# Hand-set waits, fixed buffers and two issuing engines in a batched product of 512x64 matrices

## Chip, cores and metric

Each run is on one core of one Trainium2 chip. The metric is the device time of one execution in microseconds (us); a median stands with the lowest and highest run.

## The reference

```python
x, y: float32 [8, 12, 512, 64]
np.einsum('bhtc,bhsc->bhts', x, y).astype(np.float32)   # 96 products of 512x64 by 64x512
```

25.17 MB are read and 100.66 MB written. Each load and each store of the kernel moves 2.097 MB; there are 12 loads and 48 stores.

## The kernel before

Inputs come into one of five 16 KB-per-partition slots, are cast to bf16, mixed, and transposed by VectorE. For each of 48 results TensorE makes two PSUM tiles, ScalarE evicts them into a slot, and SyncE stores the slot. Buffers come from pools, and the framework sets the waits.

```python
slots = ctx.enter_context(tc.tile_pool(name="slots", bufs=SLOTS))          # SLOTS = 5
pmpool = ctx.enter_context(tc.tile_pool(name="pmpsum", bufs=2, space=bass.MemoryType.PSUM))
...
def result(o, otf):
    i, h = divmod(o, V)
    xT, yT = made[i]
    ot = otf.rearrange("p (r s) -> p r s", s=S)
    for k in range(0, K, 4):
        pm = pmpool.tile([P, 4, S], fp32)
        for j in range(4):
            nc.tensor.matmul(pm[:, j, :], xT[:, k + j, h, :], yT[:, h * S:(h + 1) * S], ...)
        copy(nc.scalar, ot[:, k:k + 4, :], pm)
    nc.sync.dma_start(ov[i, h], otf)
...
with tc.manual_schedule():
    for g in range(SLOTS):
        load(g)
    ...                                   # casts, mixes, loads 5 to 11, results 0 to 3
    for o in range(V, V * NH):            # results 4 to 47
        result(o, slot())
        ...
```

## Time and profile before

| | before |
|---|---|
| time, median of the first 3 runs | 301.13 us (301.11 to 301.54) |
| span of the profiled execution | 299.4 us |
| busy share PE / VectorE / ScalarE / GpSimd | 46% / 52% / 71% / 19% |
| share of the transfer engines' time in the one queue | 98.8% |
| mean rate over the span | 420 GB/s |

The two rows to read together are the last ones: no compute engine is full, the transfers are.

### The profile page before, as it was taken

What the parts mean: (1) busy time and instruction counts of PE and PEld (TensorE: products, weight loads), DVE (VectorE), ACT (ScalarE), POOL (GpSimd) and SP (SyncE); (2) the same over time, 40 slices, a digit from 0 to 9 for tenths busy, and PEclk for the clock granted to TensorE, in tenths of its full rate; (3) what the DMA queues carried; (4) which work ended last, traced back from release to release, by engine and by line L of the source; (5) the groups of instructions that cost most, each with busy time, mean ns of one, the idle gap of its engine ahead of it and who ended that gap; (6) DMA issues with size and microseconds to landing.
All of it is one profiled execution on the core that took longest, in us unless ns stands there. A gap on an engine that the chain in (4) does not pass through costs nothing.

```text
span 299.4 us, 1218 instructions
## 1 busy us (share of the span) xinstructions
PE 136.7 (46%) x377; PEld 45.3 (15%) x384; DVE 154.5 (52%) x80; ACT 211.8 (71%) x109; POOL 56.6 (19%) x38
## 2 busy tenths in 40 slices
PE   0000130555665555746666466657465756465000
PEld 0000010111222221212112122212121212121000
DVE  2259996999749592916719359086192520000000
ACT  1756576999999978686867777777777686868100
POOL 3399989991000000000000000000000000000000
PEclk9999999978799997595677776677787577676555
DMA  7999999999999999999999999999999999999995
GB/s 282 431 433 429 429 427 431 429 425 436 431 427 433 431 425 430 440 424 427 440 425 427 442 422 429 437 425 431 427 431 429 425 429 425 429 422 427 429 431 219
DMA packets 8646, 125.91 MB, mean 421 GB/s; under 512 B 960, under 2 KB 960, under 8 KB 960
## 3 DMA queue, kind: packets, MB, share of 16 engines
q1 hardware_dynamic: 8640, 125.83, 98.8%
q8 instruction: 3, 0.05, 0.1%
q14 instruction: 3, 0.02, 0.0%
HBM read 25.17 MB, written 100.66 MB: 420 GB/s over the span
## 4 chain that ended last, share of the span: by engine, by line
DMA 55%; ACT 21%; DVE 7%; issue 5%; PE 2%; ACTq 1%; SPq 0%
DMA out_dram<-slot 48%; ACT slot L66 20%; DMA slot<-in_y_dram 7%; DVE yb L68 6%; PE pm L133 2%; DVE xT L115 1%; ACT yb L66 1%; ACTq L201 1%; DVE yT L120 1%; SPq L75 0%; ACTq L66 0%; ACT xk L83 0%
## 5 line engine op out<-in xcount | busy, mean ns | idle before, releaser
L66 ACT ACTIVATE slot<-pm 128x2048 f32<-128x2048 f32 x96 | 174.2, 1887 | 44.0 <-DMA out_dram<-slot 42.3
L133 PE MATMUL pm<-yT,xT 128*128 128x512 bf16 x377 | 136.7, 504 | 137.9 <-ACT slot L66 100.8
L115 DVE STREAM_TRANSPOSE xT<-xb 128x2048 uint32<-128x2048 uint32 x12 | 46.7, 3894 | 68.4 <-PE pm L133 68.3
L133 PEld LDWEIGHTS <-xT 128*128 128x128 bf16 x384 | 45.3, 118 | 228.5 <-issue 177.8
L68 DVE COPY xb<-xk 32x2048 bf16<-32x2048 bf16 x36 | 46.9, 1303 | 0.5
L68 DVE CAST yb<-slot 64x2048 bf16<-64x2048 f32 x12 | 38.5, 3204 | 16.8 <-DMA slot<-in_y_dram 16.6
L68 POOL COPY xb<-xk 32x2048 bf16<-32x2048 bf16 x12 | 37.3, 3107 | 9.6 <-ACT xk L83 8.9
L83 ACT ACTIVATE xk<-slot 128x4096 bf16<-128x4096 f32 x6 | 21.7, 3617 | 16.1 <-DMA slot<-in_x_dram 16.1
L120 DVE STREAM_TRANSPOSE yT<-yb 128x1024 uint32<-128x1024 uint32 x12 | 23.1, 1927 | 0.0
L66 ACT ACTIVATE yb<-slot 64x2048 bf16<-64x2048 f32 x6 | 14.8, 2462 | 5.1 <-DMA slot<-in_y_dram 5.1
L68 POOL CAST yb<-slot 64x2048 bf16<-64x2048 f32 x6 | 16.8, 2808 | 1.5 <-DMA slot<-in_y_dram 1.4
L152 DVE MEMSET xb<- 128x256 uint32 x8 | 2.2, 272 | 0.9 <-PEq L190 0.9
L152 POOL MEMSET xb<- 128x128 uint32 x16 | 2.3, 210 | 0.3 <-POOLq L190 0.3
L83 ACT ACT_TABLE_LOAD x1 | 1.3, 1283 | 0.7 <-PEq L190 0.7
L190 POOL MEMSET const-float32-0.0<- 128x1 f32 x1 | 0.1, 98 | 0.2 <-issue 0.2
L190 POOL MEMSET const-float32-1.0<- 128x1 f32 x1 | 0.1, 98 | 0.0
L190 POOL MEMSET const-bfloat16-1.0<- 128x1 bf16 x1 | 0.1, 98 | 0.0
L190 POOL MEMSET const-uint8-127<- 128x1 uint8 x1 | 0.1, 98 | 0.0
## 6 DMA issues: line engine op xcount, KB each, us to landing
out_dram<-slot SPq DMA_DIRECT2D x48, 2048.0 KB, 20.6
slot<-in_x_dram SPq DMA_DIRECT2D x6, 2048.0 KB, 16.4
slot<-in_y_dram SPq DMA_DIRECT2D x6, 2048.0 KB, 20.8
```

Source lines behind the costliest of these rows:

```text
L66: nc.scalar.activation(dst, src, COPY)
L68: engine.tensor_copy(dst, src)
L83: nc.scalar.activation(xk.rearrange("p r c -> p (r c)"), src, COPY)
L115: nc.vector.transpose(xT.rearrange("p (k r e) -> p k e r", k=K, e=E), xb.rearrange("p (k e c) -> p k e c", k=K, e=E),)
L120: nc.vector.transpose(yT.rearrange("p (r j) -> p j r", r=D), yb.rearrange("p (j c) -> p j c", c=D))
L133: nc.tensor.matmul(pm[:, j, :], xT[:, k + j, h, :], yT[:, h * S:(h + 1) * S], start=True, stop=True)
L152: engine.memset(zeroed[half][:, k:k + part], 0.0)
L190: nc = _bacc.Bacc("TRN2", target_bir_lowering=False, num_devices=1)
L201: with _tile.TileContext(nc) as tc:
```

## The change

The intent: drop waits that another wait already implies, know each buffer by name, and share the issuing of stores between SyncE and ScalarE. Cut to its core:

```diff
-    slots = ctx.enter_context(tc.tile_pool(name="slots", bufs=SLOTS))
-    ...
+    slots = [sb.tile([P, K * S], fp32, name=f"slot{i}") for i in range(SLOTS)]
+    ...                                       # the other pools likewise, same counts
+    def need(name, points):                   # wait only for counts not yet known,
+        ...                                   # or not implied by another wait of the same list
+    def emit(name, make, reads=(), writes=(), dma=None): ...
+    def by_act(o):
+        return o % 3 == 2 or o >= V * NH - V
     def result(o, s):
         for k in range(0, K, 4):
-            copy(nc.scalar, ot[:, k:k + 4, :], pm)
-        nc.sync.dma_start(ov[i, h], otf)
+            emit("pe", lambda: products(o, k), ...)
+            copy("dve" if o in late else "act", ot[:, k:k + 4, :], pms[pm], ...)   # late: results 43, 47
+            if k == 0:
+                while later:
+                    store(*later.pop())       # a ScalarE store goes behind the next
+        if by_act(o):                         # result's first eviction
+            later.append((o, s))
+        else:
+            store(o, s)
-    with tc.manual_schedule():
+    with tc.tile_critical():
         ...
+        for i, name in enumerate(("dve", "pool", "dve", "pe", "act")):
+            need(name, [(f"dma{i}", ticks[f"dma{i}"])])
```

More of the change, by code (lines that the diff above doesn't have):

```diff
@@ L52 @@
     )
-    const = ctx.enter_context(tc.tile_pool(name="const", bufs=1))
-    kept = ctx.enter_context(tc.tile_pool(name="kept", bufs=NG - 1))
-    slots = ctx.enter_context(tc.tile_pool(name="slots", bufs=SLOTS))
-    tpool = ctx.enter_context(tc.tile_pool(name="tpool", bufs=2))
-    pmpool = ctx.enter_context(tc.tile_pool(name="pmpsum", bufs=2, space=bass.MemoryType.PSUM))
-    loaded, inputs, mixed, made = {}, {}, {}, {}
-    zeroed = [const.tile([P, K * E * D], u32, name=f"xb{half}") for half in range(2)]
@@ L62 @@
-    in_front = [nc.vector, nc.gpsimd, nc.vector, nc.scalar]
-    def copy(engine, dst, src):
-        if engine is nc.scalar:
-            nc.scalar.activation(dst, src, COPY)
-        else:
-            engine.tensor_copy(dst, src)
+    sb = ctx.enter_context(tc.tile_pool(name="sb", bufs=1))
+    ps = ctx.enter_context(tc.tile_pool(name="ps", bufs=1, space=bass.MemoryType.PSUM))
+    slots = [sb.tile([P, K * S], fp32, name=f"slot{i}") for i in range(SLOTS)]
+    xks = [sb.tile([P, R, C], bf16, name=f"xk{i}") for i in range(NG - 1)]
@@ new lines @@
+    ybs = [[sb.tile([P, R // 2 * D], u32, name=f"yb{h}{i}") for i in range(NG - 1 + h)] for h in range(2)]
+    xbs = [sb.tile([P, K * E * D], u32, name=f"xb{half}") for half in range(2)]
+    xTs = [sb.tile([P, K * D * E], u32, name=f"xT{i}") for i in range(2)]
+    yTs = [sb.tile([P, D * R // 2], u32, name=f"yT{i}") for i in range(2)]
+    pms = [ps.tile([P, 4, S], fp32, name=f"pm{i}") for i in range(2)]
+    engines = {"act": nc.scalar, "dve": nc.vector, "pool": nc.gpsimd, "pe": nc.tensor, "sp": nc.sync}
@@ new lines @@
+    sems, ticks, known, snaps, writer, readers = {}, {}, {e: {} for e in engines}, {}, {}, {}
+    def need(name, points):
+        best = {}
+        for p, v in points:
+            if known[name].get(p, 0) < v:
+                best[p] = max(best.get(p, 0), v)
+        for p, v in list(best.items()):
+            if any(snaps[q, w].get(p, 0) >= v for q, w in best.items() if q != p):
+                del best[p]
+        for p, v in best.items():
+            engines[name].wait_ge(sems[p], v)
+            known[name][p] = v
+            for q, w in snaps[p, v].items():
+                known[name][q] = max(known[name].get(q, 0), w)
@@ new lines, in emit @@
+    def emit(name, make, reads=(), writes=(), dma=None):
+        points = [writer[r] for r in (*reads, *writes) if r in writer]
+        points += [v for w in writes for v in readers.get(w, ())]
+        if name == "pool" and name in ticks:
+            points.append((name, ticks[name]))
+        need(name, points)
+        p, step = (name, 1) if dma is None else (f"dma{dma}", 16)
+        if p not in sems:
+            sems[p] = tc.alloc_semaphore(p)
+        make().then_inc(sems[p], step)
+        at = (p, ticks.get(p, 0) + step)
+        ticks[p] = at[1]
+        snaps[at] = {**known[name], p: at[1]}
+        if dma is None:
+            snaps[at][name] = at[1]
+        for r in reads:
+            readers.setdefault(r, []).append(at)
+        for w in writes:
+            writer[w], readers[w] = at, []
@@ L70, in slot, with copy, both @@
+    made_slots, loaded, later, late = [], {}, [], (V * NH - V - 1, V * NH - 1)
+    in_front = ["dve", "pool", "dve", "act"]
+    def copy(name, dst, src, reads, writes):
+        emit(
+            name,
+            lambda: nc.scalar.activation(dst, src, COPY)
+            if name == "act"
+            else engines[name].tensor_copy(dst, src),
+            reads,
+            writes,
+        )
+    def both(i):
+        return [("slot", i, 0), ("slot", i, 1)]
     def slot():
-        return slots.tile([P, K * S], fp32, name="slot")
+        made_slots.append(len(made_slots) % SLOTS)
+        return made_slots[-1]
@@ L73, in load @@
     def load(n):
-        loaded[n] = slot()
-        nc.sync.dma_start(loaded[n], (yv if n % 2 else xv)[n // 2])
+        i = loaded[n] = slot()
+        emit(
+            "sp",
+            lambda: nc.sync.dma_start(slots[i], (yv if n % 2 else xv)[n // 2]),
+            writes=both(i),
+            dma=i,
+        )
     def compress(n):
-        src = loaded.pop(n)
+        i = loaded.pop(n)
         g = n // 2
         if n % 2 == 0:
-            xk = kept.tile([P, R, C], bf16)
-            nc.scalar.activation(xk.rearrange("p r c -> p (r c)"), src, COPY)
-            inputs[g] = xk
+            xk = g % (NG - 1)
+            dst = xks[xk].rearrange("p r c -> p (r c)")
+            copy("act", dst, slots[i], both(i), [("xk", xk)])
@@ L85, in compress @@
             return
-        ys = src.rearrange("p (r c) -> p r c", c=C)
+        ys = slots[i].rearrange("p (r c) -> p r c", c=C)
         for half in range(2):
-            yb = kept.tile([P, R // 2 * D], u32, name=f"yb{half}", bufs=NG - 1 + half)
-            yv2 = yb.bitcast(bf16).rearrange("p (j c w) -> p j w c", j=R // 2, w=2)
+            b = g % (NG - 1 + half)
+            yv2 = ybs[half][b].bitcast(bf16).rearrange("p (j c w) -> p j w c", j=R // 2, w=2)
             for ch in range(2):
@@ L96, in compress, with mix @@
                     ),
-                )
-            mixed[2 * g + half] = yb
-    def mix(i, engine, part):
+                    both(i),
+                    [("yb", half, b, ch)],
+                )
+    def mix(i, name, part):
         g, half = divmod(i, 2)
@@ L104, in mix @@
         lo = half * 64 + u * D
-        xv2 = zeroed[half].bitcast(bf16).rearrange("p (k e c u) -> p k e c u", k=K, e=E, u=2)
+        xk = g % (NG - 1)
+        xv2 = xbs[half].bitcast(bf16).rearrange("p (k e c u) -> p k e c u", k=K, e=E, u=2)
         copy(
-            engine,
+            name,
             xv2[part * D:(part + 1) * D, :, :, :, u],
-            inputs[g][lo:lo + D, :, ch * D:(ch + 1) * D].rearrange("p (e k) c -> p k e c", k=K),
+            xks[xk][lo:lo + D, :, ch * D:(ch + 1) * D].rearrange("p (e k) c -> p k e c", k=K),
+            [("xk", xk)],
+            [("xb", half, part)],
@@ L110, in mix @@
         )
     def transposes(i):
-        xb, yb = zeroed[i % 2], mixed.pop(i)
-        xT = tpool.tile([P, K * D * E], u32)
-        nc.vector.transpose(
-            xT.rearrange("p (k r e) -> p k e r", k=K, e=E),
-            xb.rearrange("p (k e c) -> p k e c", k=K, e=E),
-        )
-        yT = tpool.tile([P, D * R // 2], u32)
-        nc.vector.transpose(
-            yT.rearrange("p (r j) -> p j r", r=D), yb.rearrange("p (j c) -> p j c", c=D)
-        )
-        made[i] = (xT.bitcast(bf16).rearrange("p (k h m) -> p k h m", k=K, h=V), yT.bitcast(bf16))
@@ L125, in result @@
-    def result(o, otf):
+        g, half = divmod(i, 2)
+        b = g % (NG - 1 + half)
+        emit(
+            "dve",
+            lambda: nc.vector.transpose(
+                xTs[half].rearrange("p (k r e) -> p k e r", k=K, e=E),
+                xbs[half].rearrange("p (k e c) -> p k e c", k=K, e=E),
+            ),
+            [("xb", half, part) for part in range(4)],
+            [("xT", half)],
+        )
+        emit(
+            "dve",
+            lambda: nc.vector.transpose(
+                yTs[half].rearrange("p (r j) -> p j r", r=D),
+                ybs[half][b].rearrange("p (j c) -> p j c", c=D),
+            ),
+            [("yb", half, b, ch) for ch in range(2)],
+            [("yT", half)],
+        )
@@ L127, in result, with products @@
+    def products(o, k):
         i, h = divmod(o, V)
-        xT, yT = made[i]
-        ot = otf.rearrange("p (r s) -> p r s", s=S)
-        for k in range(0, K, 4):
-            pm = pmpool.tile([P, 4, S], fp32)
-            for j in range(4):
-                nc.tensor.matmul(
-                    pm[:, j, :], xT[:, k + j, h, :], yT[:, h * S:(h + 1) * S], start=True, stop=True
-                )
-            copy(nc.scalar, ot[:, k:k + 4, :], pm)
-        nc.sync.dma_start(ov[i, h], otf)
+        xT = xTs[i % 2].bitcast(bf16).rearrange("p (k h m) -> p k h m", k=K, h=V)
+        yT = yTs[i % 2].bitcast(bf16)
+        for j in range(4):
+            last = nc.tensor.matmul(
+                pms[k // 4][:, j, :], xT[:, k + j, h, :], yT[:, h * S:(h + 1) * S],
+                start=True, stop=True,
+            )
+        return last
@@ new lines, in by_act, with store, result @@
+    def by_act(o):
+        return o % 3 == 2 or o >= V * NH - V
+    def store(o, s):
+        i, h = divmod(o, V)
+        name = "act" if by_act(o) else "sp"
+        emit(
+            name,
+            lambda: engines[name].dma_start(ov[i, h], slots[s]),
+            reads=both(s),
+            dma=s,
+        )
+    def result(o, s):
+        ot = slots[s].rearrange("p (r s) -> p r s", s=S)
+        for k in range(0, K, 4):
+            pm = k // 4
+            half = o // V % 2
+            emit("pe", lambda: products(o, k), [("xT", half), ("yT", half)], [("pm", pm)])
+            copy("dve" if o in late else "act", ot[:, k:k + 4, :], pms[pm], [("pm", pm)], [("slot", s, pm)])
+            if k == 0:
[5 more added lines that the diff above has]
+            store(o, s)
@@ L144, in prepare @@
             for part in range(4):
-                mix(i + 1, nc.vector, part)
-    with tc.manual_schedule():
+                mix(i + 1, "dve", part)
+    with tc.tile_critical():
         for g in range(SLOTS):
             load(g)
-        for half, engine, part in ((0, nc.vector, 256), (1, nc.gpsimd, 128)):
-            for k in range(0, K * E * D, part):
-                engine.memset(zeroed[half][:, k:k + part], 0.0)
+        for half, name in enumerate(("dve", "pool")):
+            emit(
+                name,
+                lambda: engines[name].memset(xbs[half], 0.0),
+                writes=[("xb", half, part) for part in range(4)],
+            )
         front = []
@@ L157 @@
             compress(n)
-            mix(n // 4, nc.gpsimd, n % 4)
+            mix(n // 4, "pool", n % 4)
             if n == 4:
@@ L175 @@
                 prepare(o // V + 2)
+        store(*later.pop())
+        for i, name in enumerate(("dve", "pool", "dve", "pe", "act")):
+            need(name, [(f"dma{i}", ticks[f"dma{i}"])])
 _INS = ['x', 'y']
```

## The prediction

> **What bounds the kernel now.** I read the page's slices first, to see which resource is full and for how long, then its queue part, then short windows at both ends and one long one between them.
>
> ```profile
> DMA  7999999999999999999999999999999999999995
> GB/s 282 431 433 429 429 427 431 429 425 436 431 427 433 431 425 430 440 424 427 440 425 427 442 422 429 437 425 431 427 431 429 425 429 425 429 422 427 429 431 219
> q1 hardware_dynamic: 8640, 125.83, 98.8%
> SPq L201 <- DMA out_dram<-slot: 20.0, 1, 20.0
> ```
>
> The transfer engines are at nine tenths or more in all slices but the first and last, while ScalarE, the busiest compute engine, has 71% of the span. Every byte goes through one queue, fed by SyncE. The last line, from the queue's own waits, says that after the last store was issued SyncE waited 20 us for data: all computing is over at about 278 of 299.4 us. The windows say how much is not full-rate transfer:
>
> ```profile
> 1.50:2.00 0.50, 0.00 (x0) 0.00 (x0) 0.49 (x3) 0.50 (x1) 0.50 (x6) 1.00 1.91 360
> 3.50:4.00 0.50, 0.00 (x0) 0.00 (x0) 0.00 (x0) 0.00 (x0) 0.00 (x0) 1.00 0.84 360
> 4.00:295.00 291.00, 136.69 (x377) 45.34 (x384) 152.36 (x72) 210.51 (x108) 54.06 (x18) 0.79 1.01 429
> 295.00:295.50 0.50, 0.00 (x0) 0.00 (x0) 0.00 (x0) 0.00 (x0) 0.00 (x0) 0.50 1.00 426
> 297.00:297.50 0.50, 0.00 (x0) 0.00 (x0) 0.00 (x0) 0.00 (x0) 0.00 (x0) 0.50 0.08 33
> ```
>
> The last two columns are the transfer engines' share and GB/s. From 4 to 295 us the share is 1.01 and the rate 429 GB/s without a hole. 125.83 MB at 429 GB/s is 293.3 us. The other 6 us of the span are the start (first bytes after 1.5 us, full rate by 4 us) and the end (a share under 0.2 from 295.5 to 297.5, so two or three engines finishing late, then 2 us of completion and closing waits). The reported 301.13 is 1.7 us over the span; I take that as fixed.
>
> **What the Trainium skill says.** Four places of "DMA: Bandwidth & Descriptors". "Where 436 GB/s comes from" puts the ceiling of the 16 ports at 435.2 GB/s; the trace's 429 is 98.6% of it, so it agrees, and there are at most 1.4% (4 us) to win while the queue is full. "Issuing engines are not separate DMA queues" says that transfers started by different engines run on the same 16 engines, so issuing from several only saves issue time. The trace of before has one issuing engine and can't test that; SyncE's issue time is not scarce (539 ns of about 4.9 us, below). "Queues, rings and completion order" says SyncE and ScalarE own one ring each and an engine alternates between rings that have work: a ScalarE store will get about half the rate and overtake SyncE stores. "Latency and other measured facts" gives about 600 ns to the first byte; here the first load was issued at 0.74 us and its first bytes lie in the half microsecond from 1.5, so at least 0.8 us, and I use the trace: 1 to 2 us until an issued transfer feeds most engines.
>
> **The change, part by part.** (a) *Fixed buffers, hand-set waits.* The numbers of slots (5), PSUM tiles (2) and transposed tiles (2) are the same, and so are the matmuls and copies, except that VectorE takes over the four PSUM evictions of results 43 and 47, and the 24 memset pieces become two memsets. Removed waits were on events already long past; steady ScalarE waits for a store to land (1.2 us before each pair of evictions), which is the transfer bound and stays. Worth 0. GpSimd now waits for itself before every one of its instructions: some ten more small waits, hidden unless the third mix comes late. 0.
>
> (b) *The critical section.* The order listing of the changed kernel shows one more meeting of all engines before the first load and another at the end. The start delays the first byte by perhaps 0.2 to 0.4 us (estimate; the opening barrier of before took the 0.74 us up to the first issue). At the end the per-slot waits are spread over five engines instead of SyncE alone; I count +0.1 us. Together **+0.4 us**.
>
> (c) *Every third store from ScalarE.* A store of result n with n mod 3 = 2 is now issued after the first eviction of result n+1. In steady state this costs nothing: in before, a store takes 20.6 us from issue to landing at about 4.9 us of transfer each (2.097 MB at 429 GB/s), so about four are in flight, and ScalarE has 4.9 - 3.65 = 1.2 us of slack per result, against 0.54 us of issue every third result. Working through the slots by hand with the two rings sharing, the queue still holds about one and a half stores (7 us) at its lowest. So order changes, total doesn't.
>
> It matters only where the queue is nearly empty, while the stores begin:
>
> ```profile
> 0.00:67.96 67.96, 12.23 (x28) 3.95 (x29) 50.25 (x24) 45.98 (x18) 56.34 (x38) 0.96 0.98 413
> 0.00:71.86 71.86, 15.03 (x36) 4.89 (x37) 53.68 (x25) 49.63 (x21) 56.59 (x38) 0.95 0.98 415
> 0.00:78.04 78.04, 17.80 (x44) 5.84 (x45) 59.81 (x28) 55.76 (x23) 56.59 (x38) 0.95 0.99 416
> 0.00:81.87 81.87, 20.62 (x51) 6.77 (x53) 62.57 (x30) 59.44 (x26) 56.59 (x38) 0.94 0.99 416
> ```
>
> ```profile
> 64.31 3.62 ACT L66 ACTIVATE slot<-pm 128x2048 f32<-128x2048 f32 x2
> 68.18 3.65 ACT L66 ACTIVATE slot<-pm 128x2048 f32<-128x2048 f32 x2 [0.25 <-PE pm L133]
> 71.85 2.49 ACT L66 ACTIVATE yb<-slot 64x2048 bf16<-64x2048 f32 x1
> 74.37 3.65 ACT L66 ACTIVATE slot<-pm 128x2048 f32<-128x2048 f32 x2
> 78.20 5.42 ACT L66 ACTIVATE slot<-pm 128x2048 f32<-128x2048 f32 x3 [0.18 <-PE pm L133]
> L137 SPq DMA_DIRECT2D out_dram<-slot x48: 538/539/653, 54.6 to 277.8; - x48
> ```
>
> The first fence gives the bytes moved until the ends of results 2, 3, 4 and 5 on ScalarE; the second is its timeline there, plus the duration of one store issue. At 67.96 us 14 transfers had been issued (12 loads, 2 stores): 29.36 MB, less 413 x 67.96 = 28.07 MB moved, leaves 1.29 MB, 3.0 us of work. In the same way 3.8 us at 71.86, 2.5 us at 78.04 and 3.7 us at 81.87. Store 2 now waits for the first eviction of result 3: issued at 68.18 + 1.9 = 70.1 instead of 67.96, with 3.0 - 2.1 = 0.9 us of work left and 1 to 2 us until it feeds the engines: a hole of about 0.6 us (0.1 to 1.1). Its 0.54 us issue also holds up ScalarE, which is busy without pause here: store 4 comes 0.6 us later, with 1.9 us left (plus the hole's 0.6): no hole. Store 5 comes at about 84.3 instead of 81.9, with 3.7 - 2.4 = 1.3 us left plus 0.6: barely none. Engines that run behind wait less, so I count **+0.4 us** at the end.
>
> (d) *The last four from ScalarE, two results on VectorE.* The final 20 us are draining; who issued the last bytes changes neither their number nor the rate. 0.
>
> Sum: 301.1 + 0.4 + 0.4 = 301.9. I take 301.7, because I hold some chance of a small gain from two rings.
>
> **Rivals.** *Two rings fill the small gaps.* 98.6% of the ceiling leaves room if an engine's pause between descriptors or at a store's semaphore can be covered by the other ring. For: pauses must exist somewhere in the 1.4%. Against: the share reads 1.00 to 1.02 already. If half of it came back: 2 us less, 299.5. *Interleaving two stores makes HBM or the rings slower.* For: writes to two places 1 MB or more apart are mixed per engine. Against: before, loads and stores were mixed around 55 us with 429 to 431 GB/s in those slices. At 1% it would be 304. *ScalarE becomes the bound*, because its issue waits stop the evictions behind them. Against: 71% busy, the slack above, and 13 us of queued work in steady state (2.8 stores by the same count of bytes). It would need more than 1.2 us per result; then 305 and up. *The start holes add up* instead of covering each other: store 2, 5 and 8 each lose 1 us, 304.
>
> **Range and chances.** The floor is 293.3 us of transfer plus about 6 us of start and end plus 1.7 us outside the span; nothing in the change cuts the bytes. Faster by 2% (under 295.1) would need the start and end to vanish: 1%. Slower by 2% (over 307.2) needs a repeated hole or a ring penalty over 2%: 2%. The 8-in-10 range runs from the two-ring gain with half its size (300.0) to one of the penalties nearly in full (303.6).
>
> **What would show it.** Right: share near 1.0 and 427 to 430 GB/s from 90 to 290 us; first load issued 0.2 to 0.4 us later; a dip in share between 70 and 75 us; landing times of SyncE's stores longer than 20.6 us and ScalarE's spread around 10 to 20; ScalarE still waiting for landings. Wrong: a rate over 432 or under 425 GB/s through the middle; idle transfer engines after 90 us; a tail at the end that shrinks by a microsecond or more; or a front in which the first stores come earlier because hand-set waits took something off ScalarE's path before 68 us.

## More of the kernel before

The experiments were run on four different chips, each with the kernel before beside it; a ratio below is to that kernel in the same rounds.

## The result, and the profile after

| | before | changed |
|---|---|---|
| time, median of 4 runs | 301.12 us (300.98 to 301.54) | 300.96 us (300.76 to 301.08) |
| span of the profiled execution | 299.4 us | 299.3 us |
| ScalarE busy | 211.8 us | 204.2 us |

The ratio is 0.9992, with a 95% interval of 0.9974 to 1.0009: no difference. A ratio is the mean time of one kernel's fast runs over that of the other's of the same rounds, so it is not quite the ratio of the medians.

First the slices, queues and issues of the changed kernel's page (in the issue lines: count, size, median us from issue to landing):

```profile
DMA  7999999999999999999999999999999999999995
GB/s 272 429 427 434 431 425 427 429 431 427 434 434 429 429 431 428 431 434 431 427 434 428 429 434 429 429 427 436 425 425 429 427 434 423 425 423 429 431 431 239
q1 hardware_dynamic: 6048, 88.08, 69.3%
q10 hardware_dynamic: 2592, 37.75, 29.6%
out_dram<-slot SPq DMA_DIRECT2D x30, 2048.0 KB, 17.0
out_dram<-slot ACTq DMA_DIRECT2D x18, 2048.0 KB, 14.8
```

There is a second queue, and the two shares add up to 98.9%, where one had 98.8%. The row of tenths is the same in every digit. The medians from issue to landing are below the 20.6 us of before, yet bytes per microsecond are the same: fewer stores are queued at a time, which is not a faster transfer. And 17.0 us is the median of two groups. From store 15 to 42, SyncE's stores take in turn 15.7 to 17.2 us and 21.4 to 22.4 us.

Second, ScalarE's timeline where the prediction expected a hole:

```profile
64.79 3.62 ACT L113 ACTIVATE slot<-pm 128x2048 f32<-128x2048 f32 x2
68.63 1.88 ACT L113 ACTIVATE slot<-pm 128x2048 f32<-128x2048 f32 x1 [0.21 <-PE pm L202]
68.64 0.65 ACTq L216 DMA_DIRECT2D out_dram<-slot  x1
70.41 1.87 ACT L113 ACTIVATE slot<-pm 128x2048 f32<-128x2048 f32 x1
```

The third line is store 2, issued by ScalarE's sequencer (ACTq). It goes out 0.01 us after the eviction ahead of it *begins*, not after it ends, and the next eviction follows 1.78 us after the first, about as without a store between them (3.65 us for two). The transfer share of this stretch is 1.00 (window of 68 to 72 us), and counting the transfer records, the engines did not stand in it (0.00 us).

Third, ScalarE in steady state, before and then changed:

```profile
195.40 3.65 ACT L66 ACTIVATE slot<-pm 128x2048 f32<-128x2048 f32 x2 [1.24 <-DMA out_dram<-slot]
200.35 3.65 ACT L66 ACTIVATE slot<-pm 128x2048 f32<-128x2048 f32 x2 [1.30 <-DMA out_dram<-slot]
```

```profile
189.44 1.90 ACT L113 ACTIVATE slot<-pm 128x2048 f32<-128x2048 f32 x1
194.84 1.88 ACT L113 ACTIVATE slot<-pm 128x2048 f32<-128x2048 f32 x1 [3.50 <-DMA out_dram<-slot]
194.87 0.55 ACTq L216 DMA_DIRECT2D out_dram<-slot  x1
196.61 1.87 ACT L113 ACTIVATE slot<-pm 128x2048 f32<-128x2048 f32 x1
198.70 7.42 ACT L113 ACTIVATE slot<-pm 128x2048 f32<-128x2048 f32 x4 [0.21 <-PE pm L202]
209.82 1.88 ACT L113 ACTIVATE slot<-pm 128x2048 f32<-128x2048 f32 x1 [3.71 <-DMA out_dram<-slot]
```

In brackets is the idle time ahead and what ended it. Before, ScalarE waits 1.2 to 1.3 us for a landing before each result. Changed, it waits 3.5 to 3.7 us before every third result and hardly at all before the other two: nearly the same waiting (40.8 us in all, against 42.3 before), in bunches. The reason is when stores land. Before, they land some 4.9 us apart. Changed, ScalarE's store catches up with the SyncE store ahead of it: store 28 is issued at 187.8 us and store 29 at 194.9, and they land at 209.7 and 209.6, while store 27 landed at 200.7. The order of landing hardly differs (three neighbouring pairs of the 48 stores are swapped), the spacing does.

The lines also show a price of deferring. Result 29 was evicted by 191.34 us (189.44 + 1.90), but its store went out at 194.87 us: it stood behind the wait of the eviction ahead of it in the program.

I use two counts of my own in what follows, both made from the transfer records of the traces. *Queued* at an issue is the number of loads and stores issued earlier, less the data finished by then, times 4.88 us for each. (The window views count a transfer whole where it starts, so they leave less: the prediction's 3.0 us for store 2 is 3.6 us by my count.) *Standing* is the time in which fewer than 16 transfers were in progress, per engine, summed. In steady state (170 to 230 us) 13.6 to 14.3 us are queued at each issue in the kernel before, 8.3 to 10.8 us in the changed one. At the start the first load is issued at 0.95 us instead of 0.74, and the last bytes land at 297.8 us of the span in both.

### The profile page after: what moved, and what is told of

Its sections match the earlier page's. It is cut to its first block, busy times and chain, and to the rows that moved or that the text cites. A ratio compares the mean times of both kernels' runs of the same rounds, so it can differ in the third digit from the quotient of the medians.

```text
span 299.3 us, 1170 instructions
## 1 busy us (share of the span) xinstructions
PE 131.2 (44%) x384; PEld 35.2 (12%) x384; DVE 160.8 (54%) x77; ACT 204.2 (68%) x105; POOL 56.0 (19%) x23
## 4 chain that ended last, share of the span: by engine, by line
DMA 57%; ACT 22%; PE 7%; issue 4%; DVE 3%; SPq 0%; ACTq 0%
DMA out_dram<-slot 44%; ACT slot L113 19%; DMA slot<-in_y_dram 7%; PE pm L202 7%; DMA slot<-in_x_dram 6%; DVE yb L115 2%; DVE slot L115 1%; ACT xk L113 1%; ACT yb L113 1%; SPq L131 0%; ACTq L81 0%; SPq L305 0%; SPq L245 0%
## 5 line engine op out<-in xcount | busy, mean ns | idle before, releaser
L113 ACT ACTIVATE slot<-pm 128x2048 f32<-128x2048 f32 x92 | 166.6, 1883 | 50.1 <-DMA out_dram<-slot 40.8
L202 PE MATMUL pm<-yT,xT 128*128 128x512 bf16 x384 | 131.2, 485 | 146.6 <-ACT slot L113 108.6
L202 PEld LDWEIGHTS pm<-yT,xT 128*128 128x128 bf16 x384 | 35.2, 112 | 242.1 <-ACT slot L113 141.4
L115 DVE CAST yb<-slot 64x2048 bf16<-64x2048 f32 x12 | 36.1, 3012 | 17.0 <-DMA slot<-in_y_dram 16.8
L115 POOL COPY xb<-xk 32x2048 bf16<-32x2048 bf16 x12 | 36.2, 3019 | 10.5 <-ACT xk L113 9.7
L115 DVE COPY slot<-pm 128x2048 f32<-128x2048 f32 x4 | 9.0, 2286 | 29.3 <-PE pm L202 29.3
L113 ACT ACTIVATE yb<-slot 64x2048 bf16<-64x2048 f32 x6 | 14.8, 2461 | 5.1 <-DMA slot<-in_y_dram 5.1
L115 POOL CAST yb<-slot 64x2048 bf16<-64x2048 f32 x6 | 17.8, 2968 | 1.3 <-DMA slot<-in_y_dram 0.8
L251 DVE MEMSET xb<- 128x2048 uint32 x1 | 1.8, 1765 | 1.4 <-SPq L245 1.4
L251 POOL MEMSET xb<- 128x2048 uint32 x1 | 1.8, 1804 | 0.5 <-SPq L245 0.5
## 6 DMA issues: line engine op xcount, KB each, us to landing
out_dram<-slot ACTq DMA_DIRECT2D x18, 2048.0 KB, 14.8
```

The source lines that it names most:

```text
L113: lambda: nc.scalar.activation(dst, src, COPY)
L115: else engines[name].tensor_copy(dst, src),
L202: last = nc.tensor.matmul(pms[k // 4][:, j, :], xT[:, k + j, h, :], yT[:, h * S:(h + 1) * S], start=True, stop=True,)
L251: lambda: engines[name].memset(xbs[half], 0.0),
```

## The experiments

Theory: the 16 transfer engines are full from the first microseconds to the last, so the parts of the change are hidden one by one. Rival: the parts are worth something each and cancel out. (Hand-set waits, fixed buffers and the critical section were never undone alone, so a few tenths of a microsecond that cancel among these three are not excluded. Where a cut leaves nothing deferred at the end, the last `store(*later.pop())` becomes a `while later:` loop; this is not shown.)

### One part undone at a time

**One ring.** All stores from SyncE at once.

```diff
-        return o % 3 == 2 or o >= V * NH - V
+        return False
```

> The changed kernel, but every store issued by SyncE at once. Theory (the 16 transfer engines are full from start to end, so who issues is worth nothing): 300.7 to 301.3 us, ratio to before 0.998 to 1.001, and the queued work in steady state back from 8 to 11 us to 13 us or so. Rival (two rings win 1 us that the extra barrier takes back): 301.7 us or more. Rival (two rings cost, and hand-set waits win): 300.3 us or less.

300.94 us (300.82 to 301.24, 5 runs); ratio 0.9995 (0.9981 to 1.0009). 14.2 to 14.8 us are queued through most of the steady state. As the theory said: what the second ring does to the time is nothing that 5 rounds can see, and the queue is as deep as before. The edit takes the deferral away with the second ring, but the kernel that has both rings and no deferral (below) has only 9.2 to 11.9 us queued between 170 and 230 us, so it is the split that thins the queue.

**No VectorE evictions.**

```diff
-    ..., late = ..., (V * NH - V - 1, V * NH - 1)
+    ..., late = ..., ()
```

> The changed kernel, but ScalarE evicts results 43 and 47 too. Theory: the last copies end some 20 us before the last byte lands, so moving them changes nothing: 300.7 to 301.3 us, last store issued within 2 us of the changed kernel's 280.6. Rival (the VectorE evictions shorten the tail): slower by 0.5 us or more.

300.99 us (300.79 to 301.25, 5 runs); ratio 0.9994 (0.9981 to 1.0006). The last store is issued at 280.1 us instead of 280.6. Moving those four evictions to VectorE (2.29 us each there) is worth nothing that can be seen.

**Not deferred.** ScalarE issues its store right after its own second eviction.

```diff
-        if by_act(o):
-            later.append((o, s))
-        else:
-            store(o, s)
+        store(o, s)
```

> The changed kernel, but ScalarE issues its stores right after its own second eviction instead of behind the next result's first one. Theory: ScalarE's sequencer then waits for its own eviction to end and only then dispatches the next, so every third result shows a gap of 0.5 us or more between evictions; the slack hides it and the time stays at 300.7 to 301.3 us. Rival (deferring the store is what keeps ScalarE in step, so undoing it costs): 18 stores times 0.6 us, up to 10 us slower.

301.46 us (301.16 to 301.79, 5 runs); ratio 1.0008 (0.9995 to 1.0021). ScalarE's timeline of this kernel at the same place:

```profile
68.56 0.64 ACTq L216 DMA_DIRECT2D out_dram<-slot  x1
69.31 3.65 ACT L113 ACTIVATE slot<-pm 128x2048 f32<-128x2048 f32 x2 [0.78 <-PE pm L202]
```

ScalarE is now idle for 0.78 us around its own issue, where deferring left 0.21 us. (The bracket names TensorE, as in the changed kernel; that wait accounts for about 0.2 us. Further on, from 90 to 112 us, the gap behind each issue is 0.68 us, and the engine itself is named.) That is what deferring saves, and the slack pays for it almost entirely: the median is 0.5 us above the one-ring kernel's of the same rounds, on the edge of what can be told. The records show no standing after the start (0.1 us in all), but transfers of 615.6 ns on average between 90 and 190 us instead of 612.3 ns. Some 163 transfers per engine fall into those 100 us, so 3.3 ns each are 0.5 us. Why they are longer is open.

### The delay that the prediction gave to store 2

The prediction took a deferred store to go out when the eviction ahead of it ends. Issuing behind the *second* eviction makes that delay real; it does so for every deferred store, not for store 2 alone.

```diff
-            if k == 0:
+            if k == 4:
                 while later:
                     store(*later.pop())
```

> The changed kernel, but a ScalarE store is issued behind the next result's second eviction, 1.8 us later. This is the delay (2.1 us) that the prediction gave to store 2. If the prediction's model of a hole is right: store 2 issued at about 70.4 us with 0.9 to 1.3 us of work queued, share below 0.9 in the windows between 71 and 73 us, and 0.2 to 0.6 us added at the end. Rival (first bytes come sooner after an issue than 1 us, or the engines that finish last never run dry): no time added, within 0.15 us of the changed kernel.

302.44 us (302.24 to 302.62, 5 runs); ratio 1.004 (1.0028 to 1.0053), 1.5 us over the one-ring kernel of the same rounds. Windows of this kernel (the last three columns are granted clock, transfer share and GB/s), then the long window of the changed kernel:

```profile
70.00:71.00 1.00, 0.54 (x3) 0.22 (x3) 0.73 (x1) 1.00 (x2) 0.00 (x0) 1.00 1.03 442
71.00:72.00 1.00, 0.65 (x3) 0.10 (x1) 1.00 (x1) 1.00 (x1) 0.00 (x0) 1.00 0.79 328
90.00:190.00 100.00, 56.75 (x171) 15.21 (x168) 61.51 (x36) 75.91 (x43) 0.00 (x0) 0.80 1.01 426
```

```profile
90.00:190.00 100.00, 55.30 (x174) 15.25 (x173) 62.10 (x36) 77.74 (x44) 0.00 (x0) 0.81 1.01 431
```

Store 2 goes out at 70.21 us with 1.4 us queued, and the hole is there: a share of 0.79 between 71 and 72 us. It is 0.16 us of standing, at the low end of what the prediction gave. Most of the cost is elsewhere: between 90 and 190 us the share is the same but the rate is 426 instead of 431 GB/s. The mean transfer takes 617.7 ns instead of 612.3, and 5.4 ns times 163 are 0.9 us. So neither my model (0.2 to 0.6 us from the hole) nor its rival (nothing) held. The transfers are longer from the hole on (611.0 ns from 64 to 70 us, 616.8 from 72 to 90), and that costs more than the hole itself. But the hole need not be the cause: the kernel that was not deferred has none, and its transfers are longer too (615.6 ns). Why is open.

### How much reserve is left

If the reserve is thinner, a pause of ScalarE must show it. I put copies of a dead buffer onto itself ahead of result 30.

```diff
     def result(o, s):
+        if o == 30:
+            for _ in range(3):
+                stale = xks[1].rearrange("p r c -> p (r c)")
+                copy("act", stale, stale, [("xk", 1)], [("xk", 1)])
```

(In the kernel before, the same with `inputs[1]`.)

> The kernel before with three idle in-place ScalarE copies (about 3.55 us each, 10.7 us) put ahead of the evictions of result 30. Theory: when that eviction may start about 3.7 stores are queued, 17.9 us; it needs 10.7 + 3.65 us of evictions plus about 1.3 us to reach the engines, 15.7 us, so nothing is lost: within 0.3 us of 301.1. Rival (ScalarE is on the path): 5 to 10 us slower.

> The changed kernel with the same 10.7 us in the same place. Theory: store 29 sits finished but unissued behind it and only about 8.2 us of stores are queued; 10.7 + 1.3 - 8.2 = 3.8 us of empty transfer engines: 303.5 to 305.3 us. Rival (the reserve is the same as before, since the slots are the same): within 0.3 us of 301.0.

> The changed kernel with all stores from SyncE, and the same 10.7 us. Theory (it is the split over two rings that thins the reserve, not the fixed buffers or hand-set waits): no loss, within 0.3 us of the one-ring kernel. Rival (fixed buffers thin it): 3 us or more, as for the changed kernel.

> Stores of every third result from ScalarE but issued at once, and the same 10.7 us. Store 29 is then in the queue before the stall: 8.2 + 4.9 = 13.1 us queued, but the next store needs 10.7 + 3.65 + 1.3 = 15.7 us: 2.6 us lost, 303 to 304.3 us, if the thin reserve comes from the two rings' order of landing. Rival (it comes from deferring alone): no loss, within 0.3 us of 301.

| three idle copies in | time, 4 runs | ratio to before | queued when store 30 is issued |
|---|---|---|---|
| the kernel before | 301.16 us (300.97 to 301.36) | 1.0001 | 4.7 us |
| the changed kernel | 301.06 us (300.89 to 301.08) | 0.9996 | 2.4 us |
| changed, one ring | 300.95 us (300.93 to 301.05) | 0.9994 | 4.6 us |
| changed, not deferred | 302.15 us (301.39 to 302.42) | 1.0029 | 0.9 us |

My number for the changed kernel was wrong: nothing was lost. Two things had been left out. The pause does not come on top of ScalarE's 3.5 us wait for a landing there but fills it (in the trace the copies start as soon as the previous eviction ends). And store 29, which I had put behind the whole pause, is issued at 198.7 us while the copies still run. The last column still has the order of the theory, half as much queued with two rings as with one, so a fourth copy had to tell. The kernel without deferring lost 0.65 us of standing with 0.9 us queued: an issue takes about 0.9 + 0.65 = 1.5 us until it feeds the engines (an estimate from these two numbers). That kernel has both rings too, so its 0.9 us against 4.6 us with one ring says again that the thin queue is not the deferral's.

The edit is the same with `range(4)`.

> The changed kernel with four idle copies ahead of result 30 (14.3 us). With three, store 30 was issued with 2.4 us of stores still queued (two rings) against 4.6 us (one ring). Theory of a thinner reserve: one more copy is 3.55 us, so the queue is empty 1.1 us before that store is issued and the engines stand for about 1.1 + 1.5 us, plus some at store 29 ahead of it: 303.3 to 305 us. Rival (the reserve is no thinner): as the one-ring kernel in the same call, within 0.5 us.

> The changed kernel with all stores from SyncE and four idle copies. About 4.6 - 3.55 = 1.0 us is still queued when store 30 is issued; undeferred_stall showed 0.65 us of standing engines at 0.9 us queued. So 0.3 to 1.2 us slower than without a stall: 301.3 to 302.2 us, and at least 1.5 us faster than the two-ring kernel with the same stall.

Two rings: 304.35 us (304.19 to 304.43, 4 runs), ratio 1.01 (1.0084 to 1.0115). One ring: 301.88 us (301.77 to 302.02, 4 runs), ratio 1.002 (1.0003 to 1.0036). Both lie within what was expected. Windows of the two-ring kernel, then the one-ring kernel, columns as above:

```profile
200.00:203.00 3.00, 0.00 (x0) 0.00 (x0) 0.00 (x0) 2.97 (x2) 0.00 (x0) 0.50 0.89 382
203.00:206.00 3.00, 0.00 (x0) 0.00 (x0) 0.00 (x0) 3.00 (x1) 0.00 (x0) 0.50 0.87 366
206.00:209.00 3.00, 0.85 (x2) 0.43 (x4) 0.00 (x0) 3.00 (x3) 0.00 (x0) 0.50 0.84 355
209.00:212.00 3.00, 2.71 (x7) 0.56 (x6) 0.31 (x1) 2.79 (x3) 0.00 (x0) 0.58 0.41 175
```

```profile
200.00:203.00 3.00, 0.00 (x0) 0.00 (x0) 0.00 (x0) 3.00 (x1) 0.00 (x0) 0.50 1.01 431
203.00:206.00 3.00, 0.56 (x1) 0.28 (x3) 0.00 (x0) 3.00 (x3) 0.00 (x0) 0.50 1.01 431
206.00:209.00 3.00, 2.78 (x7) 0.59 (x5) 0.00 (x0) 2.79 (x2) 0.00 (x0) 0.50 0.76 322
```

With two rings the engines run dry twice, ahead of store 29 and again ahead of store 30 (0.41 between 209 and 212 us), with one ring once and briefly. Standing between 190 and 230 us is 2.9 us against 0.65. The time differs by 2.5 us for the same pause. So this is what the split does here: it does not change the time, it takes away part of what could be lost without harm. (The pause was tried at one result, and four copies were not tried on two rings without deferral.)

### Start

**A later start.** The first load waits for VectorE's memset.

```diff
+            reads=[("xb", 0, 0)] if n == 0 else [],      # and the memsets are emitted first
```

> The changed kernel, but the first load waits for VectorE's memset, so that it is issued at about 3.3 us of the span instead of 0.95. Theory (nothing but the first and last microseconds can be changed, and every microsecond there counts in full): 301.0 + 2.3 = 303.0 to 303.6 us. Rival (a later start is caught up by slack later): under 302 us.

303.48 us (302.94 to 303.57, 5 runs); ratio 1.007 (1.0058 to 1.0083). SyncE's first issue in this kernel:

```profile
3.23 0.38 SPq L131 DMA_DIRECT2D slot<-in_x_dram  x1
```

It is 2.28 us later than in the changed kernel, the last bytes land at 300.1 us instead of 297.8, and the median is 2.5 us above the changed kernel's, which was taken in another call. Nothing is caught up.

**An earlier start.** Loads 1 and 3 from ScalarE, beside SyncE's 0, 2 and 4.

```diff
+        name = "act" if n in (1, 3) else "sp"
```

> The changed kernel, but loads 1 and 3 are issued by ScalarE beside SyncE's 0, 2 and 4, so that all five are issued by about 2.5 us of the span instead of 3.5. Theory: each transfer engine has its first load's work by 2 to 3 us anyway, so at most the slow first transfers overlap better: 300.2 to 301.1 us, more bytes moved by 5 us if it helps. Rival (the start is limited by SyncE's issues): 1 us faster, 300.0 us or less.

300.97 us (300.92 to 301.17, 5 runs); ratio 0.9995 (0.9981 to 1.0009). Windows of this kernel, then of the changed one:

```profile
0.00:5.00 5.00, 0.00 (x0) 0.00 (x0) 1.76 (x1) 1.28 (x1) 2.00 (x5) 1.00 0.64 239
60.00:62.00 2.00, 2.00 (x6) 0.47 (x5) 1.97 (x2) 1.98 (x2) 2.00 (x1) 1.00 0.76 254
```

```profile
0.00:5.00 5.00, 0.00 (x0) 0.00 (x0) 1.76 (x1) 1.28 (x1) 2.00 (x5) 1.00 0.63 187
60.00:62.00 2.00, 2.00 (x6) 0.52 (x5) 2.00 (x2) 1.98 (x2) 1.97 (x1) 1.00 0.99 418
```

By 5 us it has moved 5 x (239 - 187) = 260 KB more, 0.6 us at full rate. Around 60 to 62 us, where the queue passes from the last load to the first stores, it moves 2 x (418 - 254) = 328 KB less and the gain is gone. Some thirty transfers there take 700 to 1580 ns each. Why this kernel pays at that passage and the others hardly do isn't settled: it may be that its engines reach the first store all at once, but no run tested that.

No version beat both kernels by more than 0.1%, so none is recommended on time.

## Why the prediction was right

It forecast no change that could be told, and that held because the transfers bound both kernels. The 0.6 us that it added did not come: one of its two terms was mis-sized, the other rests on a step that failed, and the range was wide enough for both.

**The bound.** Right. 429 GB/s before and 428 to 431 after in every long window; one ring, no VectorE evictions and the split loads all end within 0.1 us of the changed kernel's median. The later start shows the other half of it: 2.3 us at the start are 2.3 us at the last byte. One reading was wrong. "Two or three engines finishing late, then 2 us of completion" comes from windows that count a transfer where it starts. By the records 10 of 16 transfers are still in progress at 295.7 us and 5 at 296.0, and the last ends at 297.84 us, 1.5 us before the span does. The sum is untouched.

**(a) Waits and buffers, 0.** Right in the sum (one ring, which keeps them, ratio 0.9995), with one thing missed: the strict rotation of slots gives load 11 the buffer of load 8, which ScalarE frees late, so load 11 is issued at 51.6 us instead of 43.5, with 5.5 us queued instead of 13.4. It was hidden, but the buffers were not "the same".

**(b) The critical section, +0.4 us.** Mis-sized. The start is 0.21 us later, the low end of my estimate. After the last byte the changed kernel takes 0.1 us less, where I had counted 0.1 more. And the 0.21 us didn't reach the end in these runs: the last bytes land at 297.8 us in both profiled executions. One profile of each can't settle so little, though: the last byte lies between 297.5 and 298.0 us in the kernels whose times agree.

**(c) Every third store, +0.4 us.** This step failed, at "Store 2 now waits for the first eviction of result 3: issued at 68.18 + 1.9 = 70.1". A DMA instruction in ScalarE's program waits for the *data* it stores, which had been finished since result 2, and otherwise only for the instruction ahead of it to be handed to the engine. It went out at 68.64 us, beside that eviction and 0.2 us after its data were finished, with 3.1 us queued: no hole, and no dip in share between 70 and 75 us (0.95 to 1.15 in windows of 1 us). "Its 0.54 us issue also holds up ScalarE" failed for the same reason; the evictions stay 1.78 us apart. With the delay that I had assumed (the store behind the second eviction) a hole does open, of 0.16 us.

The steady-state part of (c) held: the times of landing change and the total doesn't. I had worked out 7 us for the lowest queue, and 8.3 us was found. That SyncE's stores take "longer than 20.6" us is half right: the ones that a ScalarE store catches up with do (21.4 to 22.4 us), the others take 15.7 to 17.2. I had missed that fewer are queued at a time, so that the others have fewer ahead of them.

**(d) The last four, 0.** Right as far as the VectorE evictions go (without them 300.99 us).

**The rivals.** Two rings filling the small gaps: not seen, one ring is as fast. Interleaving making transfers slower: not in the changed kernel, 612.3 ns per transfer between 90 and 190 us with two rings as with one. But the three kernels with longer transfers there (614.7, 615.6 and 617.7 ns: the two that were not deferred, and the one that pops later) all have two rings, and the five with one ring lie at 612.2 to 612.7. So some orders of issue on two rings may cost up to 0.9%; no run tested that. ScalarE as the bound: no, it took three idle copies (10.9 us in the trace) in steady state without loss. Start holes adding up: there were none.

That the median lies 0.7 us below my point is about the 0.8 us of (b) and (c), which should have come to nothing.

## What to carry to other kernels

When the transfer engines read full in every slice, ask of a change only what it does to the first microseconds, the last ones and the places where the queue is nearly empty; count bytes issued less bytes moved to find these. (Two orders of issue here also came with longer transfers, by 0.5% and 0.9%; why is open.) In ScalarE's program a DMA whose data were finished went out beside the instruction ahead of it (68.64 after 68.63 us), so deferring it behind the next eviction saved the gap; it also waits for what that instruction waits for (3.5 us at 194.87). Sharing stores between two rings can leave the time as it is and still thin the reserve, which shows only when something goes late.

## What the Trainium skill lacked or had wrong

- "DMA: Bandwidth & Descriptors", "Issuing engines are not separate DMA queues": right on bandwidth (300.96 us with two issuing engines, 300.94 with one). It lacks that a split can leave less queued: 8.3 to 10.8 us against 13.6 to 14.3 before and 14.2 to 14.8 with one ring, and 304.35 against 301.88 us under the same pause.
- "Perfetto Trace Analysis", "Sequencer Loop", has what I overlooked: an engine instruction is pushed into a queue and the sequencer reads on. The trace agrees (eviction at 68.63 us, DMA behind it at 68.64). The page doesn't draw the consequence for a DMA that ScalarE issues.
- "DMA: Bandwidth & Descriptors", "Latency and other measured facts", gives about 600 ns to the first byte. The records here start 1.0 us after the first issue (0.95 to 1.98 us), and with 0.9 us queued an issue left the engines standing for 0.65 us, so about 1.5 us until it feeds them.
- No page I read has that a full queue has more than one rate: 612.3 ns per 16 KB transfer between 90 and 190 us in the changed kernel, 617.7 ns in the kernel with a short hole at 71 us, 615.6 ns in the one not deferred, which has no hole, and 615 to 617 ns between 230 and 290 us in all kernels. The cause is open.
